# A four-layer decoder on one core: where the tile of transposed tokens lies in SBUF

## The chip, the cores and the metric

The kernel runs on one core of a Trainium2 chip. A core has a matrix engine (TensorE, PE in the profile, with its weight loads in a row of their own, PEld), a vector engine (VectorE, DVE), a scalar engine (ScalarE, ACT), GpSimd (POOL) and SyncE (SP), which here only issues DMAs. The engines read and write SBUF, an on-chip memory of 128 partitions; TensorE writes its results to PSUM. The metric is the device time of one execution in microseconds. Before the change it was 1206.43 us, the median of three runs (1206.05 to 1207.25).

## The reference

The reference takes 256 tokens of 1024 numbers through four layers. Each layer has a token mixer and a squared-ReLU MLP, and each of these two sits between two RMS norms:

```python
for i in range(DEPTH):                       # DEPTH = 4
    kind, j = i % N_MIXERS, i // N_MIXERS    # stick-breaking, conv, GLA, stick-breaking
    xn = rms_norm(h, norm_gains[i, 0])
    m = mixer(xn)                            # by kind
    h = h + rms_norm(m, norm_gains[i, 1])
    f = squared_relu_mlp(rms_norm(h, norm_gains[i, 2]), ffn_w_up[i], ffn_w_down[i])
    h = h + rms_norm(f, norm_gains[i, 3])
```

All inputs are float32. Nearly all of the arithmetic is the products of the tokens with the weight matrices: 1024x3072 and 1024x1024 in a mixer (some more in the GLA layer), 1024x4096 and 4096x1024 in an MLP.

## The kernel before, in words

**Split products.** A float32 number is held as two numbers of the type float32r, `hi` (a rounded copy) and `lo` (what is missing). A product of two matrices is then three products: hi by hi, hi by lo and lo by hi. `emit_upto` (lines 191 to 205) brings each block of 512 KB of weights into a tile `raw`, lets ScalarE write `hi` and VectorE write `lo`, up to 6 blocks ahead of their use.

**The transposed tokens.** After each norm the normed tokens are transposed by TensorE (line 263), and the result is split from PSUM into the tile `xt` (line 258; `spread`, `split`, lines 222 and 223). `xt` is 128 partitions x 8 x 2 x 256 numbers: for each of 8 blocks of 128 features, the `hi` of 256 tokens and behind it the `lo`. It is 16,384 bytes per partition. It is the only operand of TensorE of that name, and it is used in three ways:

- *As the stationary operand* (`x_proj`, `up_x`, through `x_stat`): 128 tokens of one feature block, 512 bytes per partition, are loaded, and 512 columns of weights stream past. In the profile this is `acc<-hi,xt` and `acc<-lo,xt`: the tile that streams stands first, the one that is loaded second.
- *As the moving operand, 512 columns and then 256* (`w_wide`): a block of weights is loaded, and `hi` and `lo` of all tokens stream past in one matmul of 512 columns; then the `lo` of the weights is loaded, and the `hi` of the tokens streams past, 256 columns.
- *As the moving operand, 256 columns* (`w_stat_steps`): the three products one by one.

The other large products (`down` in the MLP, `out_proj`) load a tile from the pool `slots` (`s` in the profile) and stream weights of 512 columns: `acc<-hi,s` and `acc<-lo,s`. Each matmul has a weight load of its own.

**Where the tiles lie.** The tiles of the pool `const` follow each other in a partition in the order in which the kernel asks for them. Before `xt` come two halves of h, `cf`, `cr`, `mones`, `onesr` and `mhalf` (8 numbers, 32 bytes). In the built program `h`, `cf`, `cr`, `mones`, `onesr` and `mhalf` begin 128 bytes past a multiple of 512, `xt` at byte 29,856, which is 160 past one. All tiles of `raw`, `hi`, `lo` and `slots` begin 256 bytes past one.

**Order of the work.** The order of the instructions on each engine is made when the program is built, from the code's order and its priorities. It does not depend on addresses.

Of the kernel before, what the change touches and what calls it, by code (L numbers as in the profile page):

```python
# [10 lines left out]
F32R = mybir.dt.float32r  # L11
# [5 lines left out]
P = 128  # L17
D = 1024
UNIT = 1024
KT = D // P  # L20
SEQ = 256
# [40 lines left out]
def hybrid_kernel(ctx: ExitStack, tc: tile.TileContext, x, norm_gains, sb_w_qkv, sb_w_o,  # L62
# [12 lines left out]
    def pool(name, bufs, **kw):  # L75
        return ctx.enter_context(tc.tile_pool(name=name, bufs=bufs, **kw))

    cp = pool("const", 1)
# [10 lines left out]
    def nm(s):  # L89
        cnt[0] += 1  # L90
        return f"{s}{cnt[0]}"

    def T(pl, shape, dt, tag):
        return pl.tile(shape, dt, tag=tag, name=nm(tag))
# [35 lines left out]
    nc.vector.memset(mones, -1.0)  # L130
    ones_r = T(cp, [P, P], F32R, "onesr")
    nc.vector.tensor_copy(out=ones_r, in_=mones)
    mhalf = T(cp, [P, 8], F32, "mhalf")
    nc.vector.memset(mhalf, -0.5)

# [104 lines left out]
    def add_norm(accs, l, i, t, dst=None):  # L240
# [11 lines left out]
        for n, cs in enumerate([slice(0, D)] if dst is None else [slice(0, 512), slice(512, D)]):  # L252
            nc.vector.scalar_tensor_tensor(out=h[t][:, cs], in0=ag[:, cs], scalar=r, in1=h[t][:, cs], op0=ALU.mult, op1=ALU.add)  # L253
            if dst is not None:
                (nc.sync, nc.scalar)[n].dma_start(out=dst[:, cs], in_=h[t][:, cs])


    xt = T(cp, [P, KT, 2, SEQ], F32R, "xt")
    xth, xtl = xt[:, :, 0, :], xt[:, :, 1, :]

    def transposes(src, dst, n):
        for j in range(n):
# [683 lines left out]
```

## Time and profile before

| | |
|---|---|
| median of three runs | 1206.43 us |
| profiled execution, its own time | 1205.45 us |
| its span, first to last instruction | 1203.6 us |
| TensorE busy | 1180.6 us, 98% |
| VectorE busy | 803.0 us, 67% |
| ScalarE busy | 673.9 us, 56% |
| mean granted TensorE clock | 0.997 |
| HBM read | 213.01 MB, 178 GB/s over the span |

The span is the time between the first and the last instruction of the profiled execution; its own time is 1.85 us more. Busy times of different engines lie beside each other. Matmuls are pipelined: the duration of one is longer than the distance from its start to the start of the next, and it is this distance, the pitch, that adds up to the time. It is read from the start times in the timeline, or from the chain of waits, where a stretch of n matmuls is given with its length.

### The profile page before, as it was taken

Reading aid. Unit: us, or ns where it says so; the run is one execution under the profiler, and the core shown is the slowest. Engines: PE = TensorE matmul, PEld = TensorE weight load, DVE = VectorE, ACT = ScalarE, POOL = GpSimd, SP = SyncE. Lnnn points to the kernel's source line nnn. Section 1 sums busy time; section 2 is a strip of 40 time slices with the busy share of each in tenths; the row PEclk is TensorE's granted clock in tenths of the full one; section 3 lists DMA queues with packets and bytes.
Section 4 is the critical chain, followed back from the end, with each engine's and each line's share of the span. In section 5 each row is a group of like instructions: output and inputs, shape, how many; then the busy total and the mean of one; then the engine's idle time right before and its main releaser. Section 6 shows DMA issues by size and latency. Waiting matters only on the chain.

```text
span 1203.6 us, 17278 instructions
## 1 busy us (share of the span) xinstructions
PE 1180.6 (98%) x6460; PEld 1010.5 (84%) x6460; DVE 803.0 (67%) x1271; ACT 673.9 (56%) x1214; POOL 51.8 (4%) x90
## 2 busy tenths in 40 slices
PE   6999999999999999999999999999999999999997
PEld 4988888888888888888789888888888988888986
DVE  6675785665788785665756678656658666865662
ACT  5687564554565564554563656545555876654550
POOL 2000100000100100000200120000000000000000
PEclk9999999999999999999999999999999999999999
DMA  8743476666466566667564347666647352766640
GB/s 261 255 127 119 140 218 198 185 194 219 142 218 199 168 219 196 190 192 220 165 198 132 106 132 230 196 194 188 207 148 235 120 162 89 220 198 191 187 157 35
DMA packets 123079, 215.18 MB, mean 179 GB/s; under 512 B 7730, under 2 KB 85682, under 8 KB 122995
## 3 DMA queue, kind: packets, MB, share of 16 engines
q1 hardware_dynamic: 122434, 213.28, 57.2%
q8 instruction: 50, 0.82, 0.3%
q10 hardware_dynamic: 432, 0.59, 0.1%
q0 software_dynamic: 128, 0.21, 0.1%
q14 instruction: 35, 0.28, 0.1%
HBM read 213.01 MB, written 1.05 MB: 178 GB/s over the span
## 4 chain that ended last, share of the span: by engine, by line
PE 93%; DMA 2%; issue 1%; ACT 1%; DVE 1%; POOL 1%; SPq 0%; DVEq 0%; POOLq 0%; ACTq 0%
PE acc L112 68%; PE wk L112 23%; PE wk L263 2%; DMA raw<-in_gla_w_in_dram 1%; DMA h<-in_x_dram 1%; ACT s L237 0%; ACT hi L202 0%; POOL sm L232 0%; ACT s L594 0%; DVE s L280 0%; POOL s L818 0%; DVE lo L203 0%; POOL sm L229 0%; DVE h L253 0%; ACT s L831 0%
## 5 line engine op out<-in xcount | busy, mean ns | idle before, releaser
L203 DVE TENSOR_TENSOR lo<-raw,hi 128x512 fp32r<-128x512 f32 x768 | 504.9, 688 | 219.2 <-ACT hi L202 215.7
L202 ACT CAST hi<-raw 128x512 fp32r<-128x512 f32 x768 | 449.1, 619 | 327.4 <-PE acc L112 178.3
L112 PE MATMUL acc<-hi,s 128*128 128x512 f32 x1216 | 339.1, 391 | 0.0
L112 PEld LDWEIGHTS acc<-hi,s 128*128 128x128 f32 x1216 | 225.6, 188 | 45.9 <-issue 0.3
L112 PE MATMUL wk<-xt,hi 128*128 128x256 f32 (+1 forms) x1120 | 252.7, 310 | 0.0
L112 PE MATMUL wk<-xt,lo 128*128 128x256 f32 x704 | 197.0, 280 | 0.0
L112 PEld LDWEIGHTS wk<-xt,hi 128*128 128x128 f32 x1120 | 182.8, 188 | 13.4 <-issue 0.9
L112 PE MATMUL acc<-lo,s 128*128 128x512 f32 x608 | 190.1, 390 | 0.0
L112 PE MATMUL acc<-xt,hi 128*128 128x512 f32 x512 | 179.3, 392 | 0.0
L112 PE MATMUL acc<-hi,xt 128*128 128x512 f32 x576 | 167.1, 403 | 0.9 <-ACT xt L222 0.9
L112 PE MATMUL acc<-xt,lo 128*128 128x256 f32 x512 | 143.5, 280 | 0.0
L112 PEld LDWEIGHTS acc<-lo,s 128*128 128x128 f32 x608 | 114.0, 188 | 23.8
L112 PEld LDWEIGHTS wk<-xt,lo 128*128 128x128 f32 x704 | 132.4, 188 | 0.2 <-issue 0.2
L112 PEld LDWEIGHTS acc<-hi,xt 128*128 128x128 f32 x576 | 108.1, 190 | 26.2 <-ACT xt L222 1.3
L112 PEld LDWEIGHTS acc<-xt,hi 128*128 128x128 f32 x512 | 96.1, 188 | 21.1
L112 PEld LDWEIGHTS acc<-xt,lo 128*128 128x128 f32 x512 | 96.3, 188 | 0.9
L112 PE MATMUL acc<-lo,xt 128*128 128x512 f32 x288 | 92.3, 400 | 0.0
L112 PEld LDWEIGHTS acc<-lo,xt 128*128 128x128 f32 x288 | 54.6, 191 | 12.9
L250 DVE TENSOR_TENSOR s<-acc,s 128x1024 f32<-128x1024 f32 (+1 forms) x16 | 19.1, 1191 | 58.8 <-ACT s L237 58.8
L229 POOL TENSOR_SCALAR sm<-sm 128x1 f32<-128x1 f32 (+1 forms) x32 | 14.3, 448 | 1011.0 <-ACT s L237 1006.3
L112 PE MATMUL acc<-s,s 128*128 128x256 f32 (+3 forms) x316 | 51.5, 336 | 2.5 <-ACT s L594 1.8
L112 PEld LDWEIGHTS acc<-s,s 128*128 128x128 f32 (+1 forms) x316 | 37.0, 167 | 13.2 <-ACT s L594 5.5
(111 smaller groups left out, 835.6 us busy)
## 6 DMA issues: line engine op xcount, KB each, us to landing
raw<-in_ffn_w_up_dram SPq DMA_DIRECT2D x128, 512.0 KB, 4.0
raw<-in_ffn_w_down_dram SPq DMA_DIRECT2D x128, 512.0 KB, 3.7
raw<-in_sb_w_qkv_dram SPq DMA_DIRECT2D x48, 512.0 KB, 5.0
raw<-in_conv_w_in_dram SPq DMA_DIRECT2D x24, 512.0 KB, 4.4
raw<-in_gla_w_in_dram SPq DMA_DIRECT2D x24, 512.0 KB, 4.5
s<-in_norm_gains_dram SPq DMA_DIRECT2D x16, 512.0 KB, 5.1
raw<-in_sb_w_o_dram SPq DMA_DIRECT2D x16, 512.0 KB, 3.7
raw<-in_conv_w_out_dram SPq DMA_DIRECT2D x8, 512.0 KB, 3.6
```

The source lines that it names most:

```text
L112: nc.tensor.matmul(out=o, lhsT=l, rhs=r, start=start, stop=stop, skip_group_check=True)
L202: nc.scalar.copy(out=hi[:, cs], in_=raw[:, cs])
L203: nc.vector.tensor_tensor(out=lo[:, cs], in0=raw[:, cs], in1=hi[:, cs].bitcast(F32), op=ALU.subtract)
L229: nc.gpsimd.tensor_scalar(out=v, in0=ss, scalar1=EPS, scalar2=None, op0=ALU.add)
L250: nc.vector.tensor_tensor(out=ag[:, cs], in0=a, in1=g[:, cs], op=ALU.mult)
L263: nc.tensor.transpose(out=dst[:, j * P:(j + 1) * P], in_=src[:, j * P:(j + 1) * P], identity=ident)
```

## The change

`xt` is asked for a few lines earlier, ahead of `mhalf` and not behind it. In the built program `xt` begins at byte 29,824, which is 128 past a multiple of 512, and `mhalf` moves behind it, to byte 46,208, also 128 past one. Every other tile keeps its address. The instructions are the same 10,640, in the same order on every engine, with the same shapes and the same waits; only the addresses of these two tiles differ.

```diff
     ones_r = T(cp, [P, P], F32R, "onesr")
     nc.vector.tensor_copy(out=ones_r, in_=mones)
+
+    xt = T(cp, [P, KT, 2, SEQ], F32R, "xt")
+    xth, xtl = xt[:, :, 0, :], xt[:, :, 1, :]
     mhalf = T(cp, [P, 8], F32, "mhalf")
     nc.vector.memset(mhalf, -0.5)
...
-
-    xt = T(cp, [P, KT, 2, SEQ], F32R, "xt")
-    xth, xtl = xt[:, :, 0, :], xt[:, :, 1, :]
-
     def transposes(src, dst, n):
```

## Rows read from the trace of the kernel before

**Rows 1.** Page, part 1: engine, busy us, share of the span, instructions.
```profile
PE 1180.6 (98%) x6460; PEld 1010.5 (84%) x6460; DVE 803.0 (67%) x1271; ACT 673.9 (56%) x1214; POOL 51.8 (4%) x90
```

**Rows 2.** Waits of PE: us in total, times, longest.
```profile
PE wk L263 <- DVE s L280: 3.3, 2, 2.7
...
PE wk L263 <- DVE s L838: 1.4, 2, 1.2
PE acc L112 <- ACT xt L222: 0.9, 1, 0.9
```

**Rows 3.** Groups by line and form: busy us, mean ns | idle before.
```profile
L112 PE MATMUL wk<-xt,lo 128*128 128x256 f32 x704 | 197.0, 280 | 0.0
...
L112 PE MATMUL acc<-xt,hi 128*128 128x512 f32 x512 | 179.3, 392 | 0.0
L112 PE MATMUL acc<-hi,xt 128*128 128x512 f32 x576 | 167.1, 403 | 0.9 <-ACT xt L222 0.9
L112 PE MATMUL wk<-xt,hi 128*128 128x256 f32 x832 | 152.1, 281 | 0.0
...
L112 PE MATMUL wk<-xt,hi 128*128 128x512 f32 x288 | 100.7, 392 | 0.0
...
L112 PE MATMUL acc<-lo,xt 128*128 128x512 f32 x288 | 92.3, 400 | 0.0
```

**Rows 4.** Timeline of PE, xt stationary: start us, us, engine, line, operation, count.
```profile
30.02 0.63 PE L112 MATMUL acc<-lo,xt 128*128 128x512 f32 x2
30.49 1.09 PE L112 MATMUL acc<-hi,xt 128*128 128x512 f32 x4
...
35.62 0.63 PE L112 MATMUL acc<-lo,xt 128*128 128x512 f32 x2
```

**Rows 5.** Chain of waits, in order of time: start us, us, what.
```profile
189.46 5.55 PE wk L112 x32
...
282.95 29.93 PE acc L112 x132
...
327.19 12.59 PE acc L112 x54
...
1070.69 5.63 PE wk L112 x48
```

**Rows 6.** Stretch: us, busy by engine, granted clock, DMA share, GB/s.
```profile
18.40:21.40 3.00, 3.00 (x9) 2.42 (x8) 3.00 (x6) 3.00 (x7) 0.00 (x0) 0.50 0.47 119
```

**Rows 7.** Timeline of PE, from 256-column matmuls into an MLP `down` stretch.
```profile
1076.16 0.63 PE L112 MATMUL acc<-hi,s 128*128 128x512 f32 x2
1076.63 0.62 PE L112 MATMUL acc<-lo,s 128*128 128x512 f32 x2
1077.09 0.39 PE L112 MATMUL acc<-hi,s 128*128 128x512 f32 x1
```

**Rows 8.** Timeline of PE, 256 columns without xt: GLA decays, then attention logits.
```profile
632.72 1.60 PE L112 MATMUL acc<-s,s 128*128 128x256 f32 x12
634.16 0.28 PE L112 MATMUL wk<-xt,hi 128*128 128x256 f32 x1
...
636.77 1.11 PE L112 MATMUL acc<-s,s 128*128 128x256 f32 x8
637.72 0.40 PE L112 MATMUL wk<-xt,hi 128*128 128x256 f32 x2
...
73.37 0.51 PE L112 MATMUL acc<-s,s 128*128 128x256 f32 x3
73.72 0.39 PE L112 MATMUL acc<-cr 128*128 128x256 f32 x2
```

**Rows 9.** Timeline of PE, attention: two logits of 512 columns, no xt.
```profile
71.48 0.63 PE L112 MATMUL acc<-s,s 128*128 128x512 f32 x2
71.95 0.28 PE L112 MATMUL acc<-cr 128*128 128x256 f32 x1
```

**Rows 10.** Timeline of PE, attention suffix: columns 256 and 512, then 256.
```profile
103.39 0.51 PE L112 MATMUL acc<-s,cr 128*128 128x256 f32 x2
103.73 0.28 PE L112 MATMUL acc<-s,onesr 128*128 128x256 f32 x1
103.85 0.51 PE L112 MATMUL acc<-s,cr 128*128 128x256 f32 x2
```

## The prediction, made before the changed kernel ran

> **What bounds the kernel now.** I read the busy shares first: TensorE works for 98% of the span, and no other engine comes near that [rows 1]. Then its waits, because a busy engine can still stand behind another: the three that have to do with what comes before or after a product with xt are 3.3, 1.4 and 0.9 us in five places [rows 2]. So the time is TensorE's pitch, matmul by matmul, and whatever an address can do to the end it does by way of that pitch. Then the groups by form, for the counts of matmuls that touch xt [rows 3]:
>
> - xt stationary, 512 weight columns moving: 576 + 288 = 864.
> - xt moving, 512 columns and then 256: 512 + 288 = 800 pairs.
> - xt moving, 256 columns alone: 832 + 704 - 288 = 1248 (the 288 are the second halves of pairs that are written to `wk`).
>
> Their mean durations there are of pipelined matmuls and no price, so the last view is the distance of starts, in the timeline and the chain. With xt stationary there are 24 matmuls from 30.02 to 35.62 us, 233.3 ns each [rows 4]; 54 in the chain at 327.19 us take 12.59 us, 233.1 ns each [rows 5]. The same work with a tile of `slots` stationary takes 29.93 us for 132, 226.7 ns each [rows 5]. Both stream the same `hi` and `lo` tiles, 512 columns, over 512 bytes of weights per partition, and into the same two PSUM banks in turn. What differs is where the stationary operand lies. All tiles but xt begin at a multiple of 64 bytes; xt, at 160 past a multiple of 512, begins 32 bytes past one. After the change it begins at a multiple of 64 too. That is the only reason in this trace for the time to move at all: nothing is added, removed or moved in the order, no wait is new and none goes.
>
> **Term 1, xt stationary.** If 226.7 ns becomes the pitch here too, each matmul gives back 6.6 to 6.7 ns. Not all do. At the start TensorE runs at a granted clock of 0.50, its level of 1.2 GHz [rows 6]: the nine matmuls of that stretch, and as many before it that I count with them, are set by the clock, so I take 20 off: 844 x 6.67 ns = 5.6 us. A stretch does not reach 226.7 at once: when TensorE goes from 256 columns to `down`, the first four matmuls take 0.93 us, 231 to 233 ns each, 0.02 us more than four at 226.7 [rows 7]. There are some 32 such entries (eight products, two halves of the tokens, each cut once by the transposes): 0.6 us. And two of TensorE's waits lie behind products with xt, 0.6 us in the 3.3 and 1.2 us in the 1.4 [rows 2]; TensorE would come there about 0.3 us earlier and wait that much longer: 0.6 us. Term 1 is 5.6 - 0.6 - 0.6 = 4.4 us less.
>
> It is a bound from one side only if address is the cause. The other bound is nothing (rival 1), and below nothing if 128 is worse than 160 (rival 2). I take the full value because the two stretches in [rows 5] differ in nothing else that I can name, and because operands that lie at 128 past a multiple of 512 are in the trace: in the attention suffix the stationary operands are `cr` and `onesr`, and 256, 512 and 256 columns take 103.39 to 103.85 us, 0.46 us. By the steady pitches of 226.7 and 120 (below) that is 0.467 us, with 6.7 ns more for the long one 0.473.
>
> **Term 2, xt moving in pairs.** In the chain 32 matmuls, 16 pairs, take 5.55 us, 346.9 ns a pair [rows 5]. With 226.7 for the long one and 120 for the short one an aligned pair would be 346.7. So there is almost nothing to gain: 800 x 0.2 ns = 0.2 us, and another 0.2 us where the stretch behind starts without the 0.02 us of [rows 7] in some of its places. Ends: nothing and 1.0 us. Taken: 0.4 us less.
>
> **Term 3, xt moving, 256 columns alone.** Now 48 take 5.63 us, 117.3 ns each [rows 5]. Aligned operands in matmuls of 256 columns are in the trace in three places [rows 8]: twelve in a row in 1.44 us, 120 ns each; eight in 0.95 us, 118.8; three in 0.35 us, 117. None is faster than what xt shows now. So the change may cost here: up to 1248 x 2.7 ns = 3.4 us. On the other side, half of the 226.7 of a matmul of 512 columns would be 113.3, 1248 x 4.0 ns = 5.0 us less. I take 118, between the three and the eight, since most of these matmuls are mixed with other work in the attention layers as those are: 1248 x 0.6 = 0.8 us more.
>
> **The rest at nothing.** ScalarE and VectorE write xt 32 times each and TensorE waited for that once, 0.9 us [rows 2]; a write that changed by a few ns changes nothing. GpSimd reads `mhalf` at the same distance past a multiple of 512 as before. The DMAs do not touch either tile. VectorE and ScalarE have a third of their time free [rows 1] to feed weights that are eaten 3% faster in a few stretches; if they could not, up to the whole of term 1 would turn into waits for `hi` and `lo`.
>
> **Sum.** -4.4 - 0.4 + 0.8 = -4.0 us. Of the profiled execution's own time, 1205.45 us, that leaves 1201.45; the median of the runs lies 0.98 us above that execution, so I predict 1202.4 us.
>
> **Where the Trainium skill speaks against it.** By the Trainium skill ("TensorE: Matmul & The Clock Gate", Step-by-step: what each phase is for) TensorE has two independent read ports in SBUF, and loading the next weights takes nothing from the matmul that runs. A stationary operand's address would then not show in a pitch that the moving one sets, and term 1 would be nothing. By the Trainium skill ("SBUF — State Buffer", Specifications (TRN2)) SBUF is read in lines of 16 bytes; 160 and 128 are both multiples of 16, so by that too the change would be none. The rows of 233 against 227 agree with neither as they stand; no run here says yet what they come from.
>
> **Rivals.**
>
> *1. Nothing changes: 1206.4 us.* Cause would be something else about xt than its distance from a multiple of 64: the part of the memory it lies in, or a start that never settles because of how these loops mix. For it: in the attention, two logits of 512 columns, all operands at multiples of 64, take 0.47 us, 235 ns each [rows 9], so a slow pitch exists without xt. Against it: such slow stretches end after a few matmuls [rows 7], with xt they last for 54 [rows 5]. Chance 0.17.
>
> *2. Slower: 1209.6 us.* What counts is how many blocks of 256 bytes the 512 bytes of a stationary operand touch: from 256 it is two, from 160 three, and from 128 still three. Then 233.3 stays, term 1 is nothing, while the 256-column matmuls with xt moving, now at a multiple of 64, settle at 120 ns as the twelve do [rows 8]: 1248 x 2.6 = 3.2 us more. It decides from the point at which the 256-column pitch rises by more than (4.4 + 0.4) / 1248 = 3.8 ns or term 1 fails. Against it stands [rows 10]. Chance 0.10.
>
> *3. Half of the gain is given back: 1204.8 us.* Term 1 and 2 come as said, and all 256-column matmuls settle at 120: -4.8 + 3.2 = -1.6 us. Chance 0.14.
>
> *4. Twice the gain: 1196.7 us.* The 256-column matmuls go to 113.3: -4.8 - 5.0 = -9.8 us. No row shows such a pitch. Chance 0.07.
>
> **How the numbers follow.** The forecast has 0.52; its own range, from term 3 between nothing and 118.8 and term 1 between 3.7 and 5.6, is 1200.5 to 1203.9. With rivals 1 and 3 the chance reaches 0.83, and that gives the range: 1199.8 us, as the forecast with no loss in any term has it (5.6 + 1.0 = 6.6 less), to 1207.0, no change and half a microsecond of spread. Outside are rivals 2 and 4. A change of under 0.2%, 2.4 us, is about what a measurement of this kernel cannot tell from none. Faster by more than that: most of the forecast's 0.52, rival 4's 0.07 and a little of rival 3, 0.60. Within: the rest of rival 3, most of rival 1 and the edge of the forecast, 0.28. Slower: rival 2 and a tail of rival 1, 0.12.
>
> **What would show it.** In the profile after, the stretches of `acc<-hi,xt` and `acc<-lo,xt`: 226.7 ns from start to start shows term 1, 233 refutes it and with it the forecast. The pairs at 347 ns: term 2. The 48 matmuls of the last MLP's 256-column stretches in 5.6 to 5.7 us: term 3; 5.76 is rival 3, 5.44 rival 4. TensorE's waits for `hi` and `lo` must stay at nothing, or the weights come too late for the faster pitch.

## The result, and the profile after

The changed kernel takes 1210.63 us (median of ten runs, 1209.17 to 1211.25), against 1207.33 us for the kernel before (ten runs, 1204.72 to 1208.36). The ratio is 1.003, with a 95% interval from 1.0021 to 1.0039: 0.3% slower, where 0.33% faster was forecast. Measured again beside the experiments below, the kernel before had medians of 1205.97, 1206.3 and 1206.53 us.

The page after, part 1, and TensorE's waits (as in [rows 1] and [rows 2]; lines after are 1 lower or 3 higher than before):

```profile
PE 1184.6 (98%) x6460; PEld 1014.1 (84%) x6460; DVE 803.5 (66%) x1271; ACT 673.9 (56%) x1214; POOL 53.3 (4%) x90
```

```profile
PE wk L262 <- DVE s L277: 9.0, 1, 9.0
PE wk L262 <- DVE s L279: 4.4, 2, 3.0
...
PE wk L262 <- DVE s L837: 1.2, 1, 1.2
```

TensorE is still busy for 98%, and it waits for the same instructions as before. The first of these waits, 9.0 us for the first tokens to arrive, was 8.1 in the profiled execution of before:

```profile
PE wk L263 <- DVE s L278: 8.1, 1, 8.1
```

The second went from 3.3 [rows 2] to 4.4 us. These two are 2.0 of the 5.9 us by which the spans of the two profiled executions differ (1203.6 and 1209.5); the rest is in the pitch. The timeline of PE after with xt stationary, which answers to [rows 4]:

```profile
29.52 0.62 PE L112 MATMUL acc<-lo,xt 128*128 128x512 f32 x2
...
35.09 0.64 PE L112 MATMUL acc<-lo,xt 128*128 128x512 f32 x2
```

24 matmuls in 5.57 us: 232.1 ns each, where 233.3 was and 226.7 was forecast. The chain of waits after, which answers to [rows 5] (with two attention stretches and one with both pairs and products of slots, 16.48 us, ahead, which were not shown before):

```profile
57.77 9.39 PE wk L112 x79
...
75.53 9.49 PE wk L112 x80
...
174.74 16.48 PE acc L112 x80
...
191.22 5.62 PE wk L112 x32
...
285.24 29.93 PE acc L112 x132
...
329.43 12.54 PE acc L112 x54
...
1075.57 5.76 PE wk L112 x48
```

The same three stretches in the chain of before:

```profile
56.35 9.38 PE wk L112 x79
...
74.11 9.39 PE wk L112 x80
...
173.02 16.44 PE acc L112 x80
```

| products | before, ns | after, ns | count | change by the starts, us |
|---|---|---|---|---|
| slots stationary, 512 columns | 226.7 | 226.7 | 1824 | 0 |
| xt stationary, 512 columns | 233.1 | 232.2 | about 830 | -0.8 |
| xt moving, pair of 512 and 256 | 346.9 | 351.3 | 800 | +2.9 |
| xt moving, 256, last MLP | 117.3 | 120.0 | 288 | +0.8 |
| xt moving, 256, attention and GLA | 117.4 | 118.6 | 960 | +0.8 |
| transposes, with the waits at them | | | 224 | +1.1 |

Each pitch is that of one stretch of the chain by its count (12.54 us by 54, 5.62 by 16 pairs, 5.76 by 48, 9.49 by 80). The last column is not worked out from it: there the distances from each start to the next are added up over both traces, matmul by matmul in the same order, without the first 36, some of which run at the granted clock of 0.50 of [rows 6]. It is less than pitch by count where other stretches of a kind moved less: the pairs that are written to `acc` (16 of them and 48 products of slots go from 16.44 to 16.48 us), or an attention stretch that took 118.7 ns before and takes 118.9 now (79 in 9.38 and 9.39 us). The column adds up to 4.8 us, and with 0.8 us at the first start and 0.2 in other work and single waits to the difference of the two spans. The products alone are 3.7 us of it. The medians differ by 3.3 us, 2.5 to 4.7 by the interval. They differ less than the spans: the profiled execution of before is one of its faster ones, that of after the slowest of its ten.

### The profile page after: what moved, and what is told of

Read it like the earlier page. It is cut to its first block, busy times and chain, and to the rows that moved or that the text cites. A ratio compares the mean times of both kernels' runs of the same rounds, so it can differ in the third digit from the quotient of the medians.

```text
span 1209.5 us, 17278 instructions
## 1 busy us (share of the span) xinstructions
PE 1184.6 (98%) x6460; PEld 1014.1 (84%) x6460; DVE 803.5 (66%) x1271; ACT 673.9 (56%) x1214; POOL 53.3 (4%) x90
## 4 chain that ended last, share of the span: by engine, by line
PE 93%; DVE 2%; DMA 2%; issue 1%; ACT 1%; POOL 1%; SPq 0%; DVEq 0%; POOLq 0%; ACTq 0%
PE acc L112 67%; PE wk L112 23%; PE wk L262 2%; DMA raw<-in_sb_w_qkv_dram 1%; DVE lo L206 1%; DMA h<-in_x_dram 1%; POOL sm L232 0%; ACT s L240 0%; POOL sm L235 0%; ACT s L593 0%; DVE s L279 0%; POOL s L817 0%; ACT hi L205 0%; DVE h L256 0%; ACT s L830 0%
## 5 line engine op out<-in xcount | busy, mean ns | idle before, releaser
L112 PE MATMUL wk<-xt,hi 128*128 128x256 f32 (+1 forms) x1120 | 255.6, 311 | 0.0
```

The lines of the kernel that those rows point to most:

```text
L112: nc.tensor.matmul(out=o, lhsT=l, rhs=r, start=start, stop=stop, skip_group_check=True)
```

## The experiments

The theory at first was rival 2's, that the stationary operand's own place counts (*blocks*). Against it stood *distance*: what counts is how far apart the loaded and the streaming operand of a matmul begin, modulo some power of two. Later *own place* was set against distance: that a moving operand is quick at 32 past a multiple of 64.

### A kernel of matmuls alone, and three decoders

**pitch.** Matmuls in sections, two tiles, every section with its own two starts:

```diff
+    for r in (256, 160, 128, 0, 32, 64, 96, 192, 224, 288, 320, 384, 448):
+        section("h", r, 256, 48)          # kind, stationary at, moving at, matmuls
+    for r in (128, 0, 160, 384):
+        section("h", r, r, 48)
...
+    for r in (256, 160, 128, 0, 64, 96, 192, 384):
+        section("p", 256, r, 48)
```

> This kernel leaves all of the decoder out: it runs only matmuls on normally distributed float32r numbers, in sections of 48 or 72, and the pitch of each section is read from its starts. Letters: s is where the stationary operand begins, m where the moving one does, a to p for 0 to 480 bytes past a multiple of 512 in steps of 32. Sections h have 512 moving columns, p pairs of 512 and 256, q 256. Three theories. Blocks (rival 2 of the prediction): what counts is how many blocks of 256 bytes the 512 bytes of a stationary operand touch; with the moving one at 256, the stationary one at 256 and 0 gives 226.7 ns, every other place 231 to 234. Distance: a steady pitch needs both operands at the same distance past a multiple of 512; 226.7 for s = m wherever that is (256 with 256, 128 with 128, 0 with 0, 160 with 160), 231 to 234 for all others. Place: the address within 512 bytes has nothing to do with it and all sections h take one pitch. For q with the stationary at 256: 120 where the moving one is at 256 by the first two theories, 119 at 128 and 117.5 at 160 as in the decoder before and after the change.

Its chain of waits: start us, us, section, count.

```profile
25.63 10.89 PE h_si_mi L96 x48
36.51 11.20 PE h_sf_mi L96 x48
47.72 11.20 PE h_se_mi L96 x48
58.91 10.91 PE h_sa_mi L96 x48
...
170.20 10.91 PE h_se_me L96 x48
181.12 10.89 PE h_sa_ma L96 x48
192.01 10.93 PE h_sf_mf L96 x48
...
213.85 8.47 PE p_si_mi L96 x48
222.32 8.34 PE p_si_mf L96 x48
230.66 8.43 PE p_si_me L96 x48
...
281.35 8.62 PE q_si_mi L96 x72
...
298.42 8.54 PE q_si_me L96 x72
...
324.08 8.48 PE q_si_mc L96 x72
```

The letters i, f, e, a and c are 256, 160, 128, 0 and 64; h has 512 columns, p pairs, q 256 columns. 10.89 us by 48 is 226.9 ns, 11.20 is 233.3. Quick are 256 with 256, 0 with 256, 128 with 128, 0 with 0 and 160 with 160: all whose distance is a multiple of 256, at 32 past a multiple of 64 too (226.9 to 227.7 ns). Slow are 160 and 128 with 256. Blocks falls with 128 and 128 (three blocks, quick), my multiple of 64 with 128 and 256 (slow) and with 160 and 160 (quick). For pairs it is the other way round: distance 0 takes 8.47 us, 352.9 ns a pair; with the moving operand 96 bytes before the stationary one (160 and 256) a pair takes 347.5, with 128 before 351.3. These are the decoder's pitches before and after to within 0.6 ns. With 256 columns, distance 0 takes 8.62 us for 72, 119.7 ns, and 128 before takes 118.6.

**xt256, all128, xt0.** The changed kernel with unused tiles around xt. For xt256:

```diff
+    T(cp, [P, 32], F32, "pad")
     xt = T(cp, [P, KT, 2, SEQ], F32R, "xt")
+    T(cp, [P, 96], F32, "tail")
```

all128 has only the tile behind (96 numbers), xt0 has 96 ahead and 32 behind.

> The decoder with xt at 256 past a multiple of 512, as hi, lo, raw and slots are; these lie 512 bytes further than before. Blocks and distance both: products with xt stationary go to 226.7 ns (48 to 54 of them in a row at 227), pairs to 346.7, matmuls of 256 columns alone to 118 to 120: against the kernel before 793 x 6.8 ns = 5.4 us less and 1248 x 1.5 to 2 ns = 2 to 2.5 us more, some 3 us less, 0.25%, and some 6 us less than the kernel with xt at 128. Place: no different from the kernel with xt at 160, 0 us.

> The decoder with every large tile, xt too, at 128 past a multiple of 512: xt where the changed kernel has it, all others moved there. Distance: as with all at 256, products at 226.7 ns with xt stationary and with slots stationary, some 3 us less than before. Blocks: now the tiles of slots touch three blocks of 256 bytes too, and the 1824 matmuls of 512 columns with slots stationary go from 227 to 232 or 233 ns as well: 9 to 12 us more than the changed kernel, 1220 us. Place: as the changed kernel, 3 us more than before.

> The decoder with xt at a multiple of 512, all other large tiles at 256 past one. Blocks: two blocks of 256 bytes per stationary operand, 226.7 ns with xt stationary, some 3 us less than before. Distance: not the same distance from a multiple of 512, xt stationary stays at 231 to 234 ns, and the time at that of before or of the change, 0 to 3 us more than before. If it is the distance from a multiple of 256 that must be the same, as with blocks. Place: 0 us.

| kernel | xt, other tiles | us | ratio to before, interval |
|---|---|---|---|
| xt256 | 256, 256 | 1211.46 | 1.0044 (1.003 to 1.0058) |
| all128 | 128, 128 | 1210.86 | 1.0038 (1.0025 to 1.0051) |
| xt0 | 0, 256 | 1210.73 | 1.0036 (1.0023 to 1.005) |

All three are slower than before, and no theory had expected that of xt256. Its chain, and that of all128:

```profile
190.50 5.65 PE wk L112 x32
...
329.44 12.27 PE acc L112 x54
...
1074.50 5.76 PE wk L112 x48
```

```profile
192.16 5.65 PE wk L112 x32
...
286.74 29.99 PE acc L112 x132
...
1019.61 12.26 PE acc L112 x54
```

With xt stationary 54 take 12.27 us, 227.2 ns: what distance had said, also with everything at 128, where the 132 with slots stationary stay at 227.2 as well (blocks had said 232 for them). What I had wrong is the pair: 5.65 us by 16 is 353.1 ns, not 346.7. The distance that is best with xt stationary is among the worst for the pairs. Added up over the starts as above, xt stationary takes 4.7 us less in xt256 than before, the pairs 4.0 and the 256 columns 2.6 us more, and the transposes with the waits at them 1.9 us more.

### One distance at a time

Here hi and lo tiles get 64 numbers more, and only the blocks that are loaded as weights (256 columns wide; those of the products in which xt moves) are put further in. The tiles are then 4352 bytes long and begin at odd and even multiples of 256 in turn, which changes no distance modulo 256. For split96:

```diff
-            hi = T(hip, [P, UNIT], F32R, "hi")
-            lo = T(lop, [P, UNIT], F32R, "lo")
+            o = 24 if b == 256 else 0
+            hi = T(hip, [P, UNIT + 64], F32R, "hi")[:, o:o + UNIT]
+            lo = T(lop, [P, UNIT + 64], F32R, "lo")[:, o:o + UNIT]
```

with xt at 256. undo_mov has 56 for the 24 and xt at 128; mov_only has 8 and xt at 160. rel96 has no such edit: a tile of 120 numbers behind xt puts all others at 224.

> The decoder with xt at 128 past a multiple of 512 as in the changed kernel, and raw, hi, lo and slots at 224, so that xt lies 96 bytes before them as in the kernel before. Theory distance (what the section kernel points to: the pitch follows from how far the two operands of a matmul lie apart, modulo 256 bytes): all pitches as before, 233.4 ns with xt stationary, pairs at 347 to 348, 256 columns at 117 to 119, and the time of before, within 0.15%. Theory own place (a moving operand streams at 117.3 ns per 256 columns where it begins 32 past a multiple of 64, and slower at a multiple of 64, whatever the other operand does): xt at 128 is as slow as in the changed kernel, 3 to 5 us more than before.

> The decoder with xt at 256, and of hi and lo only the blocks that are loaded as weights (the 256-column blocks, for the products in which xt moves) begin 96 bytes later in their tiles, at 352 past a multiple of 256 or 512; the blocks that stream past xt or slots stay at 256. Distance: xt stationary at distance 0, 226.7 to 227.6 ns (5 us less than before), and the products in which xt moves keep the 96 bytes of before, pairs at 347 to 348, 256 columns at 117 to 119: in all 4 to 5 us less than before, 0.35 to 0.4%, faster than both kernels. Own place: xt moves from 256, pairs at 352.8 and 256 columns at 119.9 as in the kernel with xt at 256, 4 to 5 us more than before.

> The changed kernel (xt at 128), only that the blocks of hi and lo that are loaded as weights begin 224 bytes later in their tiles, so that xt, where it moves, lies 96 bytes before them again; where xt is stationary nothing is undone. Distance: pairs back at 347 to 348, 256 columns back at 117 to 119, xt stationary stays at the 232.4 ns of the changed kernel: the time of before, 0 to 1 us less. Own place: as the changed kernel, 3 to 5 us more than before.

> The other half of the change alone: xt at 160 as before, so that it is stationary at the distance of before, and the blocks of hi and lo that are loaded as weights begin 32 bytes later, so that xt, where it moves, lies 128 bytes before them as in the changed kernel. Distance: pairs at 351, 256 columns at 118.7 to 120, xt stationary at 233.4: 4 us more than before, 0.3%. Own place: xt moves from 160 as before, nothing changes against before.

| kernel | xt before the weights that stream | xt before the weights that are loaded | us | ratio to before, interval |
|---|---|---|---|---|
| before | 96 | 96 | 1206.3 | |
| rel96 | 96 | 96 | 1206.37 | 0.9999 (0.999 to 1.0008) |
| undo_mov | 128 | 96 | 1206.92 | 1.0005 (0.9996 to 1.0014) |
| mov_only | 96 | 128 | 1211.7 | 1.0045 (1.0032 to 1.0057) |
| split96 | 0 | 96 | 1204.09 | 0.998 (0.9971 to 0.9989) |

rel96 has xt where the changed kernel has it, at 128, and the time of before: the place is not the cause, the distance is, and own place falls. undo_mov and mov_only split the change: the distance with xt moving makes all of the loss (mov_only), and putting it back takes all of it away (undo_mov; a difference from before of more than 0.14% is outside its interval). The chain of mov_only has the pairs nearly as after and the 256 columns of the last MLP at 118.5 ns, though their distance is the 128 that gives 120.0 there after; that of rel96 has both as before:

```profile
191.11 5.61 PE wk L112 x32
...
1075.55 5.69 PE wk L112 x48
```

```profile
191.27 5.55 PE wk L112 x32
...
1071.74 5.63 PE wk L112 x48
```

split96 sets each distance by itself and is 0.2% faster than the kernel before:

```profile
189.00 5.55 PE wk L112 x32
...
326.82 12.27 PE acc L112 x54
```

Its pitches are those expected. By the starts, xt stationary takes 4.7 us less than before; 2.2 us came. TensorE's transposes of the next tokens stand at fixed places in its order, behind products with xt stationary, and it now comes to them before VectorE has normed the tokens. The transposes before, and in split96 (in groups by form: busy us, mean ns | idle before):

```profile
L263 PE MATMUL wk<-cf,s 128*128 128x128 f32 x224 | 30.7, 280 | 13.3 <-DVE s L278 8.1 <-DVE s L280 3.3 <-DVE s L838 1.4
```

```profile
L265 PE MATMUL wk<-cf,s 128*128 128x128 f32 x224 | 30.7, 281 | 14.2 <-DVE s L280 8.1 <-DVE s L282 3.8 <-DVE s L840 1.6
```

The waits by line, of which [rows 2] has two times for L280:

```profile
PE wk L265 <- DVE s L282: 3.8, 4, 2.7
...
PE wk L265 <- DVE s L444: 0.3, 2, 0.2
```

The idle time is 0.9 us more. By the starts, the transposes with the intervals that lead up to them take 1.9 us more, most of it in nine places between the last product with xt stationary and the first transpose. The 1824 products of slots take 0.5 us more; why, and what else differs between executions, stays open.

### Is there a better distance?

**pitch2.** As pitch, with the stationary operand at 256 and the moving one d bytes behind it:

```diff
+    for kind, count in (("h", 48), ("p", 48), ("q", 72)):
+        for d in range(0, 256, 16):
+            section(kind, d, count)
```

> This kernel leaves all of the decoder out, as the section kernel before it: sections h (512 moving columns), p (pairs of 512 and 256), q (256), with the stationary operand at 256 past a multiple of 512 and the moving one d bytes further, d from 0 (da) to 240 (dp) in steps of 16. Theory distance modulo 256 gives, from the first section kernel and the decoder: h 226.7 at 0, 229 at 64, 233 to 234 at 32, 96, 128 and 160; q 120 at 0 and 96, 118.7 at 128, 117.3 at 160, 117.8 at 32, 64 and 192; p 356 at 0, 353.6 at 128, 349.6 at 160. A rival reading is that only whole steps of 64 or 32 matter, and that 16 more or less leaves a pitch where it is; by distance in lines of 16 bytes each step has a pitch of its own. Open is 224, and whether any distance brings pairs below 347 or 256 columns below 117.

The prices of pairs in this expectation are 2 to 3 ns too high: by the chain of pitch they are 352.9, 351.3 and 347.5. Its own chain:

```profile
25.34 10.88 PE h_da L93 x48
36.22 11.12 PE h_db L93 x48
...
170.11 11.26 PE h_dn L93 x48
...
192.56 10.88 PE h_dp L93 x48
203.45 8.33 PE p_da L93 x48
...
371.83 8.16 PE q_de L93 x72
...
397.26 8.16 PE q_dh L93 x72
```

The letters a, b, e, h, n and p are 0, 16, 64, 112, 208 and 240 bytes. With 512 columns 0 and 240 are quick (226.7 ns), 16 already is not (231.7), and 208 is the slowest (234.6): steps of 16 bytes count. Of the pairs no section came below 346.7. Of the 256 columns two did at 8.16 us, 113.3 ns: d of 64 and 112. But the moving operand at 64 and the stationary one at 256, which is 64 behind modulo 256, had taken 117.8 in pitch (8.48 us by 72), and pairs at distance 0 take 347.1 here (8.33 by 24) and had taken 352.9 there. The two sections of pairs have the same two starts. So one distance has more than one steady pitch.

**best64, best112.** split96, with another offset for the weights of the 256-column products alone:

```diff
-            o = 24 if b == 256 else 0
+            alone = key[0][1] in ("q", "k") or key[0][0] == DEPTH - 1 and key[0][1] == "up" and key[0][-1] == 1
+            o = 0 if b != 256 else 48 if alone else 24
```

best112 has 36 for the 48.

> The decoder as in the kernel with xt at 256 and the weight blocks of the moving-xt products 96 bytes later, only that the blocks for the products of 256 columns alone (q and k of attention and GLA, the second half of each up-group of the last layer) begin 192 bytes later, so that xt moves 64 bytes after them. In the second section kernel that distance gave 113.3 ns, in the first one 117.8. If the pitch is a matter of the distance alone, 113.3: 1248 x 4 to 4.6 ns = 5 to 5.7 us less than that kernel, 1198.5 us. If a distance has several steady pitches and the one taken depends on how the stretch is entered, anything from 113.3 to 120: 1198 to 1206 us. If 113.3 holds only where each matmul has a stationary operand of its own (in w_stat the same weights are loaded for two in a row, which changes no distance), 117 to 120 and no gain.

> The same with 144 bytes, so that xt moves 112 bytes after the weights of the 256-column products: 113.3 ns in the second section kernel. Distance alone: 1198.5 us, as with 64. Several steady pitches: 1198 to 1206.

best64 takes 1203.28 us, ratio 0.9969 (0.9957 to 0.9981), the fastest of all; whether it beats split96's 0.998 the intervals leave open. best112 takes 1205.1 us, 0.9988 (0.9979 to 0.9997). Of the 5 us there is hardly anything. Two like stretches of the second attention layer in the chain of best64:

```profile
953.69 9.42 PE wk L112 x80
...
972.04 9.07 PE wk L112 x80
```

Products of the same kind at the same distance modulo 256 take 117.8 ns in one and 113.4 in the other. Two pitches exist in one run, and the slower one is the usual one here. The kernel before has two as well: the 118.7 ns (79 in 9.38 us) and 117.4 ns (80 in 9.39 us) shown above are both at 96, and there all weight tiles begin at one place past a multiple of 512. What chooses between them is open.

## Why the prediction was wrong

**What bounds the kernel** was right: in the products it was TensorE's pitch that moved, 3.7 us, and the time with it.

**The step that failed** is the reading of [rows 5]: "what differs is where the stationary operand lies", and its 32 bytes past a multiple of 64 as the cause. The two stretches differ in the distance between their operands too, 96 against 0 modulo 256, and the trace of before had no long stretch in which place and distance came apart, for all weight tiles lie at one place. rel96, with xt at 128 and the time of before, and the sections 160 with 160 and 128 with 256 of pitch show that it was the distance.

**Term 1**, 4.4 us less, became 0.8 less: the change takes the distance with xt stationary from 96 to 128, and not to 0. With 0 the pitch of 227.2 is there (xt256, split96), 5.7 ns a matmul and 4.7 us less by the starts, so the size of the term was right for another change. (Its 6.67 ns is a little high: its own rows give 6.4 to 6.6. Its eight products are nine, 864 being nine times 96; that is 0.1 us.) The attention suffix that I called on for 128 [rows 10] has operands 128 apart as well; its 0.46 us were too short a stretch to tell a steady pitch.

**Term 2**, 0.4 us less, became 2.9 us more, the largest part of the loss. I made an aligned pair out of 226.7 and 120, pitches of two other sequences. In sequence they take 353 ns at distance 0 in the decoder (xt256), and 351.3 at the changed kernel's 128.

**Term 3**, 0.8 us more, became 1.6. That the rows at 118 to 120 [rows 8] came near is in part luck: their operands are at distance 0, those of the changed kernel 128 apart, which gives 119.7 and 118.6 ns in pitch. The counts leave out 24 matmuls of 256 columns in the GLA layer that take a tile of slots as weights.

**The absorbed part** of term 1, 0.6 us, was too small: split96 has 1.9 us more at the transposes, and some 2.5 us missing in all.

**The rivals.** Rival 2 had the side and nearly the time, 1209.6, but by luck: of its price for the 256 columns half was there, the blocks of 256 bytes are refuted by all128, and the pairs, the largest part, were in no rival. Rival 1's two slow logits [rows 9] have operands at distance 0 as well as at multiples of 64, so the distance does not explain them either; that they are a start that had not settled was argued and not shown.

By the Trainium skill ("TensorE: Matmul & The Clock Gate", Step-by-step: what each phase is for) weights are loaded through a read port of their own and take no bandwidth from the matmul that runs. The sections of pitch do not agree with that as it stands: 226.9 and 233.3 ns differ in nothing but the two starts.

## What to carry to other kernels

Where TensorE sets the time, read its pitch by kind of product, from the chain or from starts, and compare kinds that do the same work: 227 against 233 ns was plain in the trace. Before such a difference is put down to where one operand lies, look for a pair of kinds in which the place differs and the distance to the other operand does not, or make one in a kernel of matmuls alone, which told in one run what the decoder could not. A layout that is good for one kind of product can be bad for the next, so the offsets belong to the blocks of each kind and not to the tile that they share.

## What the runs showed that was not expected

- The pitch of float32r matmuls with 512 columns goes from 226.7 ns to as much as 234.6 ns with the distance between the starts of the loaded and the streaming operand, modulo 256 bytes; with the streaming one 16 bytes behind it is 231.7 ns, with 16 before still 226.7. With 256 columns it lies between 113.3 and 120 ns, and distance 0, the best for 512 columns, gives 120, among the slowest.
- A pair of 512 and 256 columns takes 346.7 to 353 ns, and its order of distances is not that of either half.
- A distance can have two steady pitches: 113.4 and 117.8 ns in one run of best64, 117.4 and 118.7 ns in the kernel before, 347.1 and 352.9 ns for pairs at distance 0 in the two section kernels. Why the memory or the engine does this no run shows.
